# Operands of a feed-forward block's second weight matrix prepared beside the mixers instead of in the feed-forward stage, on one Trainium2 core

## The chip, the cores and the metric

The kernel runs on one core of a Trainium2 chip. The core has a matrix engine (PE, with its weight loads shown apart as PEld), a vector engine (DVE), a scalar engine (ACT), a general engine (POOL), and a sync engine (SP) that issues most of the DMAs. Each engine works through its own list of instructions in order. The metric is the device time of one execution, in microseconds (us), and lower is better.

## The reference

One decoder layer, run for a prompt of 2048 tokens behind 16 meta tokens, and for 8 sample sequences of 4 tokens, with the same weights. The mixer has three groups of heads side by side: HGRN2 (a gated linear recurrence), mLSTM, and sliding-window attention with sinks. A SwiGLU block follows.

```python
def _trunk(h, init_states, past_kvs, params):
    ...
        y, st = _mixer(_rmsnorm(h, norm_mix[l]), p, init_states[l], kv)
        h = h + y
        h = h + _swiglu(_rmsnorm(h, norm_ffn[l]), w_ffn_in[l], w_ffn_out[l])
    ...
def _swiglu(hn, w_ffn_in, w_ffn_out):
    g, u = jnp.split(hn @ w_ffn_in, 2, axis=-1)
    return (jax.nn.silu(g) * u) @ w_ffn_out
```

The model width is 1024, the inner width of the SwiGLU block is 2816, and all inputs are float32. The results are the two trunk outputs and the recurrent states of both groups.

## The kernel before

**Stages.** Tokens are worked in 17 tiles: tile 0 holds the 32 sample tokens and the 16 meta tokens, tiles 1 to 16 hold 128 prompt tokens each. For each tile `project` multiplies by the input weights, which stay in SBUF, and `mix` runs the three mixers. `mixer_prompt` (L857) takes turns between three generators, `swa_prompt`, `mlstm_prompt` and `hgrn_prompt`. In HGRN2 a chain of levels doubles its block length each time: PE products `lv` (L527), a masked copy on DVE (L540), and updates of `qz` and `k` on DVE (L549, L551). After the tiles come the output product, the sample group's mixer and the norm of the feed-forward block. Then follow three groups of six tiles (the third with the short tile 0 and four others) through the SwiGLU block.

**Numbers as pairs.** A float32 operand is held as a sum of two float16 values: `split_w` (L154 to L156) writes the high part on ACT and the low part on DVE, and a product takes three float16 passes (`PASSES`).

**Seven products for eight.** The SwiGLU block uses a Strassen-like scheme: a 2 by 2 block product with seven products and sums of blocks. A unit of 256 columns of weights is therefore seven operands, each as a float16 pair, 896 KB in all. The sums are four subtractions or additions on POOL (`left` L1012 for the first matrix, `right` L1020 for the second), and the split takes three calls of `split_w` (`operands`).

**Group 0 makes, groups 1 and 2 load.** In the first group (6 buffers `w`) `kept` (L1127) makes a unit from the raw weights and stores it to a DRAM scratch (L1134); in the other groups (11 buffers) it loads it from there (L1136). There are 44 units of the first matrix (`gu_operands`, raw loads L1186) and 22 of the second (`dn_operands`, raw loads L1198, scratch `wdn_scratch`).

**Inside a group.** The 11 inner blocks `jq` are taken in four parts of 2, 3, 3 and 3 (`PARTS`). `hidden` does the gate and the up product of a block (`quad`, PE products L1239; POOL sums L1248, L1249), then the product of the two (DVE L1262) and the block sums (POOL L1274 to L1280), and writes the pairs `hh` (ACT L1268, DVE L1269). `down` (PE products L1292) needs the `hh` of a whole part and the units of the second matrix, `m` = 0 and 1, and adds to `xr`. In the first two parts of group 0 `prep_late` also prepares the inputs of the last tiles.

**Order.** The instructions are written in program order; a scheduler with a timeline of its own then places each on its engine's list, earlier where it judges the operands ready and the engine free. Buffers from pools bound how far: a new tile of a tag waits until the oldest one of that tag is released. DMAs on SP are a list like any other.

**Sample group.** Tile 0's projection leaves the sample group's results (`s_q`, `s_k`, `s_cin` and so on, in `tl` and beside it) in SBUF tiles of their own until the sample mixer reads them after tile 15.

**Masks.** Seven masks `lv`, 64 wide, are made by two `affine_select` each (L406, L407).

## Time and profile before

| | |
|---|---|
| median of 3 runs | 2424.07 us (2414.37 to 2427.03) |
| profiled execution, its own time | 2414.44 us |
| span of its trace | 2412.7 us |
| granted PE clock, mean | 0.97 |
| mixers of tiles 1 to 15 | about 100 to 784 us of the span |
| SwiGLU group 0, first to last PE product | 1055.3 to 1595.9 us |
| SwiGLU group 1 | 1602.1 to 2056.4 us |
| SwiGLU group 2 | 2056.2 to 2394.6 us |

How to read the rows shown below. A row of a group of instructions gives line, engine, operation, output and inputs with their shapes, then count, busy time in us, mean duration in ns, and the engine's idle time just before them with what ended it. A row of a table of stretches gives, after the stretch and its length, the busy us (and the count of instructions) of PE, PEld, DVE, ACT and POOL, then the granted PE clock, the share of time for which the DMA engines were busy, and GB/s. A row of waits gives who waited for whom, us in total, times, and the longest. A row of the timeline gives start, duration, engine, line and instruction, and in brackets the idle time before. Line numbers are those of the kernel before.

### The profile page before, as it was taken

Reading aid. Unit: us, or ns where it says so; the run is one execution under the profiler, and the core shown is the slowest. Engines: PE = TensorE matmul, PEld = TensorE weight load, DVE = VectorE, ACT = ScalarE, POOL = GpSimd, SP = SyncE. Lnnn points to the kernel's source line nnn. Section 1 sums busy time; section 2 is a strip of 40 time slices with the busy share of each in tenths; the row PEclk is TensorE's granted clock in tenths of the full one; section 3 lists DMA queues with packets and bytes.
Section 4 is the critical chain, followed back from the end, with each engine's and each line's share of the span. In section 5 each row is a group of like instructions: output and inputs, shape, how many; then the busy total and the mean of one; then the engine's idle time right before and its main releaser. Section 6 shows DMA issues by size and latency. Waiting matters only on the chain. (4 is left out here: it accounts for less than half of the span.)

```text
span 2412.7 us, 51978 instructions
## 1 busy us (share of the span) xinstructions
PE 2220.3 (92%) x20298; PEld 1607.4 (67%) x20298; DVE 1679.2 (70%) x4030; ACT 943.5 (39%) x2526; POOL 1211.7 (50%) x1629
## 2 busy tenths in 40 slices
PE   6989999999999899896989979889999999999996
PEld 6677767767776445444657556567686767888886
DVE  8788988988988756558879677746454535655546
ACT  7554455554554432334343434422212123332323
POOL 7344344444443464549778788744232324544435
PEclk9999999999999899997999989899999999999998
DMA  7232333333223755996436545684324247744441
GB/s 258 50 63 69 66 67 68 75 61 74 66 64 73 173 183 192 275 330 222 153 139 231 196 158 191 191 287 185 148 108 168 108 152 199 269 176 175 177 174 38
DMA packets 294329, 364.95 MB, mean 151 GB/s; under 512 B 203808, under 2 KB 234480, under 8 KB 294067
## 3 DMA queue, kind: packets, MB, share of 16 engines
q1 hardware_dynamic: 285090, 331.02, 43.6%
q0 software_dynamic: 4384, 15.93, 1.7%
q10 hardware_dynamic: 4608, 14.68, 1.7%
q8 instruction: 159, 2.61, 0.4%
q14 instruction: 88, 0.71, 0.1%
HBM read 212.24 MB, written 103.50 MB: 131 GB/s over the span
## 5 line engine op out<-in xcount | busy, mean ns | idle before, releaser
L1239 PE MATMUL s<-x,w 128*128 128x384 f16 (+1 forms) x5544 | 826.4, 312 | 14.8 <-DMA w<-wgu_scratch 6.2
L1239 PEld LDWEIGHTS <-w 128*128 128x128 f16 x5544 | 542.6, 98 | 296.5 <-issue 13.8
L1292 PE MATMUL dn<-w,hh 128*128 128x256 f16 (+1 forms) x4158 | 444.4, 278 | 56.0 <-ACT hh L1268 23.6
L1292 PEld LDWEIGHTS <-hh 128*128 128x128 f16 (+1 forms) x4158 | 379.6, 99 | 119.8 <-ACT hh L1268 27.8
L212 PEld LDWEIGHTS <-xT 128*128 128x128 f16 (+1 forms) x1992 | 177.4, 99 | 191.4 <-issue 25.2
L1268 ACT ACTIVATE hh<-tmp 128x384 f16<-128x384 f32 (+1 forms) x231 | 112.4, 494 | 280.4 <-DVE tmp L1262 164.5
L1248 POOL TENSOR_TENSOR tmp<-tmp,tmp 128x384 f32<-128x384 f32 (+1 forms) x66 | 65.3, 990 | 279.0 <-ACT tmp L1247 271.8
L1269 DVE TENSOR_TENSOR hh<-tmp,hh 128x384 f16<-128x384 f32 (+1 forms) x231 | 144.5, 633 | 74.2 <-ACT hh L1268 72.5
L212 PE MATMUL wo<-wo,xT 128*128 128x512 f16 x768 | 180.8, 394 | 9.5 <-DVE xn L992 4.6
L156 DVE SCALAR_TENSOR_TENSOR w<-raw,w 128x512 f16<-128x512 f32 (+1 forms) x136 | 111.9, 855 | 7.0 <-ACT w L155 6.9
L1250 DVE TENSOR_TENSOR tmp<-s,tmp 128x384 f32<-128x384 f32 (+1 forms) x66 | 34.2, 518 | 107.3 <-PE s L1239 107.3
L212 PE MATMUL d<-xT,qf 128*128 128x128 f16 (+1 forms) x1632 | 107.7, 220 | 0.0
L156 DVE SCALAR_TENSOR_TENSOR w<-sums,w 128x1024 f16<-128x1024 f32 x68 | 96.9, 1427 | 11.4 <-ACT w L155 11.4
L1259 ACT ACTIVATE tmp<-tmp 128x384 f32<-128x384 f32 (+1 forms) x132 | 61.6, 489 | 107.9 <-DVE tmp L1250 52.6
L212 PE MATMUL d<-xT,bqk 128*128 128x128 f16 (+1 forms) x1632 | 100.6, 221 | 3.2 <-DVE e L278 3.2
L1324 DVE SCALAR_TENSOR_TENSOR xr<-dn,xr 128x256 f32<-128x256 f32 x192 | 78.7, 417 | 34.4 <-PE dn L1292 30.2
L212 PEld LDWEIGHTS <-qf 128*128 128x128 f16 x1632 | 94.4, 100 | 9.1 <-issue 4.1
L212 PEld LDWEIGHTS <-bqk 128*128 128x128 f16 x1632 | 94.0, 100 | 5.4 <-issue 4.5
L212 PE MATMUL d<-xT,cq 128*128 128x128 f16 (+1 forms) x1632 | 96.2, 217 | 0.0
L212 PE MATMUL d<-bvo,xT 128*128 128x512 f16 (+1 forms) x408 | 96.2, 380 | 0.0
L1262 DVE SCALAR_TENSOR_TENSOR tmp<-tmp,tmp 128x384 f32<-128x384 f32 (+1 forms) x132 | 71.9, 558 | 34.1 <-POOL tmp L1249 32.6
L212 PE MATMUL d<-aig,xT 128*128 128x512 f16 (+1 forms) x408 | 92.4, 379 | 3.4 <-DVE g L358 3.4
(536 smaller groups left out, 4064.6 us busy)
## 6 DMA issues: line engine op xcount, KB each, us to landing
w<-wgu_scratch SPq DMA_DIRECT2D x88, 896.0 KB
wgu_scratch<-w SPq DMA_DIRECT2D x44, 896.0 KB
w<-wdn_scratch SPq DMA_DIRECT2D x44, 896.0 KB
raw<-in_w_ffn_in_dram SPq DMA_DIRECT2D x88, 256.0 KB
...
xs<-in_x_prompt_dram SPq DMA_DIRECT2D x26, 512.0 KB
...
raw<-in_w_ffn_out_dram SPq DMA_DIRECT2D x22, 512.0 KB
```

Of the source, the lines that this page charges most:

```text
L156: V.scalar_tensor_tensor(lo, src, scale, hi, op0=ALU.mult, op1=ALU.subtract)
L212: T.matmul(out, lh(k, a), rh(k, b), start=(n == 0), stop=(n == 3 * nk - 1))
L1239: T.matmul(out, A[k // 2][p][:, a, k % 2 * P : k % 2 * P + P], x2[r][:, k // 2, op, k % 2, :n], start=i == 0, stop=i == 11)
L1248: G.tensor_tensor(r12, r12, r22, op=ALU.add)
L1250: V.tensor_tensor(r11, prod(A12, B21), r11, op=ALU.add)
L1259: S.activation(d, d, AF.Silu, scale=UF)
L1262: V.scalar_tensor_tensor(d, v, UF * HS, d, op0=ALU.mult, op1=ALU.mult)
L1268: S.activation(hi, v, AF.Copy)
L1269: V.tensor_tensor(lo, v, hi, op=ALU.subtract)
L1292: T.matmul(out, hh[p][:, q, a, off : off + L], ws[q][r][:, b], start=(q, p, r) == order[0], stop=(q, p, r) == order[-1])
L1324: V.scalar_tensor_tensor(x[:L, cc], m, UD, x[:L, cc], op0=ALU.mult, op1=ALU.add)
```

## The change

The units of the second matrix are no longer made in group 0. They are cut into 44 pieces of half a unit (`wdn_scratch` gets one more axis), and a new generator `dn_prep(4)` runs as a fourth beside the three mixers in tiles 4 to 14. Each piece is loaded raw one piece ahead (three DMAs into a tile `nr`, two buffers), goes through four POOL subtractions into `ns` (one buffer) and two `split_w` calls into `nw` (one buffer), and is stored by one DMA. In all three SwiGLU groups `dn_operands` now loads a unit with two DMAs, and PE reads it as two runs of 128 columns.

To make room, the sample group's projections are written into tiles of the tags `nr`, `ns` and `nw`, stored to a new DRAM scratch after tile 0's projection (`put_away`, five DMAs) and loaded again before the sample mixer (`take_back`, five DMAs). The tile `tg` now shares the tag of `xq`. Five masks `lv`, 32 wide, replace the seven; each takes two `affine_select` into a scratch tile `dm` and two copies.

```diff
-    wdn_d = nc.dram_tensor("wdn_scratch", (NFF // 2, 2, P, 2 * 7 * 256), F16, kind="Internal").ap()
+    wdn_d = nc.dram_tensor("wdn_scratch", (NFF // 2, 2, 2, P, 2 * 7 * P), F16, kind="Internal").ap()
+    smp_d = nc.dram_tensor("smp_scratch", (4, P, 512), F32, kind="Internal").ap()
...
+    def pack():
+        packed[:] = [at_("nr", [P, 512], bufs=2), at_("nr", [P, 512], bufs=2), at_("ns", [P, 512]), at_("nw", [P, 896])]
...
+    def put_away():
+        for which, n, c0, c1 in SPK_PARTS:
+            nc.sync.dma_start(smp_d[which, :n, c0:c1], packed[which][:n, c0:c1])
+
+    def take_back(s):
+        pack()
+        for which, n, c0, c1 in SPK_PARTS:
+            nc.sync.dma_start(packed[which][:n, c0:c1], smp_d[which, :n, c0:c1])
+        for tag in SPK:
+            setattr(s, tag, in_pack(tag))
...
             if s.name == "s":
-                return at_("s_" + tag, shape, dt)
+                if not packed:
+                    pack()
+                return in_pack(tag)
...
-                tg = at_("tg", [P, 256])
+                tg = at_("xq", [P, 256])
...
+        if t == 0:
+            put_away()
         yield
...
-    for li in range(7):
+    for li in range(5):
         h = 1 << li
-        m = at_(f"lv{li}", [P, 64])
+        m = at_(f"lv{li}", [P, 32])
+        z = am_("dm", [P, 64])
...
+        for u in range(2):
+            G.tensor_copy(m[u * 64 : u * 64 + 64], z[u * 64 : u * 64 + 64, u * 32 : u * 32 + 32])
...
-    def mixer_prompt(s, yT, off):
+    def mixer_prompt(s, yT, off, *others):
         y = zt("y", [P, 512])
-        interleave(swa_prompt(s, yT, off), mlstm_prompt(s, y[:, 256:512]), hgrn_prompt(s, y[:, 0:256]))
+        interleave(swa_prompt(s, yT, off), mlstm_prompt(s, y[:, 256:512]), hgrn_prompt(s, y[:, 0:256]), *others)
         finish_y(y, yT, off, s.L)
+
+    dn_pieces = [(jq, m, u) for jq in range(NFF // 2) for m in range(2) for u in range(2)]
+    dn_raw = []
+
+    def dn_load():
+        if dn_pieces:
+            jq, m, u = dn_pieces.pop(0)
+            x = at_("nr", [P, 4, P], bufs=2)
...
+            nc.sync.dma_start(x[:, 0], rows[0][:, 1])
+            nc.sync.dma_start(x[:, 1], rows[0][:, 0])
+            nc.sync.dma_start(x[:, 2:4], rows[1])
+            dn_raw.append((x, wdn_d[jq, m, u]))
+
+    def dn_prep(n):
+        if not dn_raw:
+            dn_load()
+            yield
+        for _ in range(n):
+            x, dst = dn_raw.pop(0)
+            dn_load()
+            yield
+            b12, b11, b21, b22 = (x[:, i] for i in range(4))
+            s = at_("ns", [P, 4, P])
+            w = at_("nw", [P, 2, 7, P], F16)
+            G.tensor_tensor(s[:, 0], b12, b11, op=ALU.subtract)
+            G.tensor_tensor(s[:, 1], b22, s[:, 0], op=ALU.subtract)
+            G.tensor_tensor(s[:, 2], b22, b12, op=ALU.subtract)
+            G.tensor_tensor(s[:, 3], b21, s[:, 1], op=ALU.subtract)
+            split_w(x[:, 1:4], w[:, 0, 0:3], w[:, 1, 0:3], WS)
+            yield
+            split_w(s, w[:, 0, 3:7], w[:, 1, 3:7], WS)
+            nc.sync.dma_start(dst, w.rearrange("p a o c -> p (a o c)"))
+            yield
...
-            mixer_prompt(seg_of[t][0], yT, 0)
+            mixer_prompt(seg_of[t][0], yT, 0, *([dn_prep(4)] if 4 <= t < 15 else []))
...
+    take_back(sseg)
     smp = sample_mixer(tc, nc, I, O, locals())
...
     def dn_operands(jq, m):
-        def make(w):
-            raw = raw_tile()
...
-            right(w, sum_tile(), raw[:, 0], raw[:, 1], raw[:, 2], raw[:, 3], raw.rearrange("p (k h) c -> p h k c", k=2)[:, 0], WS)
-        return kept(wdn_d[jq, m], make)
+        w = w_full().rearrange("p a o c -> p (a o c)").rearrange("p (u z) -> p u z", u=2)
+        for u in range(2):
+            nc.sync.dma_start(w[:, u], wdn_d[jq, m, u])
+        return w.rearrange("p u (r o c) -> p u r o c", r=2, o=7)
...
-                T.matmul(out, hh[p][:, q, a, off : off + L], ws[q][r][:, b], start=(q, p, r) == order[0], stop=(q, p, r) == order[-1])
+                T.matmul(out.rearrange("t (u c) -> t u c", u=2), hh[p][:, q, a, off : off + L], ws[q][:, :, r, b], start=(q, p, r) == order[0], stop=(q, p, r) == order[-1])
```

What the scheduler makes of it is seen in the engines' lists. First POOL's list in group 0 of the SwiGLU block, at the end of the fourth part's products, before the change: L1249 is the second sum of the last gate product, L1248 the first of the last up product, L1274 and the next lines the block sums of `hidden`, and L1022 to L1025 the subtractions of a unit of the second matrix.

```order
L1249 TENSOR_TENSOR tmp_21519<-tmp_21519,tmp_21518 128x384
L1022 TENSOR_TENSOR sums_22127<-raw_22125 128x256
L1024 TENSOR_TENSOR sums_22127<-raw_22125 128x256
L1023 TENSOR_TENSOR sums_22127<-raw_22125,sums_22127 128x256
L1022 TENSOR_TENSOR sums_22142<-raw_22140 128x256
L1024 TENSOR_TENSOR sums_22142<-raw_22140 128x256
L1025 TENSOR_TENSOR sums_22127<-raw_22125,sums_22127 128x256
L1023 TENSOR_TENSOR sums_22142<-raw_22140,sums_22142 128x256
L1025 TENSOR_TENSOR sums_22142<-raw_22140,sums_22142 128x256
L1248 TENSOR_TENSOR tmp_21657<-tmp_21657,tmp_21659 128x384
L1249 TENSOR_TENSOR tmp_21659<-tmp_21659,tmp_21658 128x384
L1274 TENSOR_TENSOR tmp_21656<-tmp_21517,tmp_21519 128x384
```

The same place of POOL's list in the changed kernel, where L1321, L1322 and L1347 are the lines that were L1248, L1249 and L1274:

```order
L1321 TENSOR_TENSOR tmp_22001<-tmp_22001,tmp_22003 128x384
L1322 TENSOR_TENSOR tmp_22003<-tmp_22003,tmp_22002 128x384
L1321 TENSOR_TENSOR tmp_22141<-tmp_22141,tmp_22143 128x384
L1322 TENSOR_TENSOR tmp_22143<-tmp_22143,tmp_22142 128x384
L1347 TENSOR_TENSOR tmp_22140<-tmp_22001,tmp_22003 128x384
```

At this place no preparation stands any more between the sums of the gate product and those of the up product, and in the second, third and fourth part POOL's list goes from the sums of `hidden` straight to those of `down`.

Next DVE's list in the mixer of tile 4, before the change: the rows of the mLSTM stabiliser (`mb`, `mr`, `rows`) with `es` and `kx` of the attention, and a level of HGRN2 (`att`).

```order
L673 CAST mb_74_473<-mrow_4338 4x128
L821 TENSOR_TENSOR es_4365<-ng_4355,sink_457 128x8
L771 COPY mst_4544<-rows_72_471 4x1
L350 SCALAR_TENSOR_TENSOR kx_4959<-d_4910,kx_4959 64x128
L674 TENSOR_TENSOR mr_4381<-mrow_4338,mb_74_473 4x128
L675 CAST mb_74_473<-mr_4381 4x128
L676 TENSOR_TENSOR mb_74_473<-mr_4381,mb_74_473 4x128
L540 COPY_PREDICATED att_4227<-lv_43_375,lv_4343 64x4x8x4 x2
```

The same place of DVE's list in the changed kernel (L714 to L717 were L673 to L676), with L158, the low parts of a piece:

```order
L715 TENSOR_TENSOR mr_4407<-mrow_4361,mb_77_482 4x128
L323 TENSOR_SCALAR f_5660<-dd_5655 128x256
L716 CAST mb_77_482<-mr_4407 4x128
L360 SCALAR_TENSOR_TENSOR qlo_5864<-d_5765,qx_730_5862 64x512
L717 TENSOR_TENSOR mb_77_482<-mr_4407,mb_77_482 4x128
L158 SCALAR_TENSOR_TENSOR nw_9633<-nr_9050,nw_9633 128x384
L158 SCALAR_TENSOR_TENSOR nw_9633<-ns_9632,nw_9633 128x512
L815 TENSOR_SCALAR kd_4602<-pairm_438,kd_4602 4x2
```

The piece stands in tile 4's stretch, although the program writes it beside a later tile: counted over DVE's whole list, by the row of `ng` (L816 before, L857 now) that each tile has once, the 44 pieces lie 1, 4, 5, 7, 7, 5, 7, 7 and 1 in the stretches that end with the `ng` row of tile 0, 1, 2 and so on to 8. The scheduler has moved them ahead of tiles 4 to 14.

Last, SP's list in the same tile of the changed kernel: the two transposes of the attention's probabilities (`pT`, L877 for the high part and L879 for the low), which followed each other before as L836 and L838.

```order
L877 DMA_TRANSPOSE pT_4397<-ph_4396 128x8x128
L914 DMA nr_9852<-in_w_ffn_out_dram 128x128
L915 DMA nr_9852<-in_w_ffn_out_dram 128x128
L916 DMA nr_9852<-in_w_ffn_out_dram 128x2x128
L937 DMA wdn_scratch<-nw_9779 128x1792
L879 DMA_TRANSPOSE pT_4397<-ph_4396 128x8x128
```

Three raw loads and a store, each with waits of its own, now stand between them.

More of the change, by code (lines that the diff above doesn't have):

```diff
@@ L217, in trunk, with in_pack @@
         pass
+    SPK = {"q": (0, 0, 64), "k": (0, 64, 64), "f": (0, 128, 64), "cin": (0, 192, 224), "ck": (0, 416, 32), "cq": (1, 0, 128),
+           "cv": (1, 128, 128), "va": (1, 256, 256), "ga": (2, 0, 256), "gb": (2, 256, 256), "vb": (3, 0, 260), "g": (3, 260, 8)}
+    SPK_PARTS = ((0, P, 0, 448), (1, P, 0, 128), (1, NS, 128, 512), (2, NS, 0, 512), (3, NS, 0, 268))
+    SHAPES = {"q": (P, 2, NS), "k": (P, 2, NS), "f": (P, 2, NS), "cin": (P, 4, NB, 7), "cq": (P, 4, NS), "ck": (P, NS),
+              "cv": (NS, P), "g": (NS, 8), "va": (NS, 256), "ga": (NS, 256), "gb": (NS, 256), "vb": (NS, 4, 65)}
+    packed = []
+    def pack():
+        packed[:] = [at_("nr", [P, 512], bufs=2), at_("nr", [P, 512], bufs=2), at_("ns", [P, 512]), at_("nw", [P, 896])]
+    def in_pack(tag):
+        which, o, n = SPK[tag]
+        shape = SHAPES[tag]
+        v = packed[which][: shape[0], o : o + n]
+        if len(shape) == 3:
+            return v.rearrange("p (a b) -> p a b", a=shape[1])
+        return v.rearrange("p (a b c) -> p a b c", a=shape[1], b=shape[2]) if len(shape) == 4 else v
+    def put_away():
[7 more added lines that the diff above has]
+            setattr(s, tag, in_pack(tag))
     def project(t, s_out):
@@ L299, in project @@
                 if s.name == "s":
-                    s.cin = at_("s_cin", [P, 4, NB, 7])
+                    s.cin = in_pack("cin")
+                    G.memset(s.cin, 0.0)
                     S.activation(s.cin[:, :, :, 3:7], pv[:, :, sl].rearrange("p j (b t) -> p j b t", t=NT), AF.Copy, scale=US)
@@ L382, in project @@
                 if s.name == "s":
-                    s.vb = at_("s_vb", [NS, 4, 65])
+                    s.vb = in_pack("vb")
                     V.memset(s.vb[:, :, 64:65], 1.0)
@@ L401, in trunk @@
     lv = []
-    for li in range(7):
+    for li in range(5):
         h = 1 << li
-        m = at_(f"lv{li}", [P, 64])
+        m = at_(f"lv{li}", [P, 32])
+        z = am_("dm", [P, 64])
         nb = 64 // h
-        G.affine_select(out=m, in_=ones[:, :64], pattern=[[-2 * h, nb], [0, h]], compare_op=ALU.is_ge, fill=0.0, base=0, channel_multiplier=1)
-        G.affine_select(out=m, in_=m, pattern=[[2 * h, nb], [0, h]], compare_op=ALU.is_ge, fill=0.0, base=h - 1, channel_multiplier=-1)
+        G.affine_select(out=z, in_=ones[:, :64], pattern=[[-2 * h, nb], [0, h]], compare_op=ALU.is_ge, fill=0.0, base=0, channel_multiplier=1)
+        G.affine_select(out=z, in_=z, pattern=[[2 * h, nb], [0, h]], compare_op=ALU.is_ge, fill=0.0, base=h - 1, channel_multiplier=-1)
+        for u in range(2):
+            G.tensor_copy(m[u * 64 : u * 64 + 64], z[u * 64 : u * 64 + 64, u * 32 : u * 32 + 32])
         lv.append(m.bitcast(I32))
@@ L855, in put_yT @@
         V.scalar_tensor_tensor(lo, pv, scale, hi, op0=ALU.mult, op1=ALU.subtract)
-    def mixer_prompt(s, yT, off):
+    def mixer_prompt(s, yT, off, *others):
         y = zt("y", [P, 512])
-        interleave(swa_prompt(s, yT, off), mlstm_prompt(s, y[:, 256:512]), hgrn_prompt(s, y[:, 0:256]))
+        interleave(swa_prompt(s, yT, off), mlstm_prompt(s, y[:, 256:512]), hgrn_prompt(s, y[:, 0:256]), *others)
         finish_y(y, yT, off, s.L)
+    dn_pieces = [(jq, m, u) for jq in range(NFF // 2) for m in range(2) for u in range(2)]
[4 more added lines that the diff above has]
+            x = at_("nr", [P, 4, P], bufs=2)
+            rows = [w_dn[(2 * jq + k) * P : (2 * jq + k + 1) * P, m * 512 : m * 512 + 512].rearrange("p (h u c) -> p h u c", h=2, u=2)[:, :, u] for k in range(2)]
+            nc.sync.dma_start(x[:, 0], rows[0][:, 1])
[22 more added lines that the diff above has]
+            yield
     def finish_y(y, yT, off, L):
```

8 lines of the change are left out of this document (3 added, 5 removed).

## The prediction

> **What bounds the kernel now.** I read the page first (PE busy 92% of the span), then the table of stretches for the three SwiGLU groups. Groups 0 and 1 have the same products on the same shapes, and differ in that group 0 makes the weight units and group 1 loads them. The first two rows are these groups, the other eight the `down` blocks of their four parts, group 0's first.
>
> ```profile
> core 0: us, PE busy (x) PEld busy (x) DVE busy (x) ACT busy (x) POOL busy (x), PEclk, DMA share, GB/s
> 1055.30:1595.90 540.60, 477.00 (x3243) 322.55 (x3241) 414.14 (x631) 222.10 (x440) 422.37 (x437) 0.94 0.57 196
> 1602.10:2056.40 454.30, 454.01 (x3236) 317.06 (x3237) 220.44 (x428) 107.42 (x233) 153.72 (x176) 1.00 0.47 168
> ...
> 1111.80:1167.40 55.60, 35.66 (x253) 26.61 (x254) 51.16 (x77) 20.72 (x42) 50.84 (x52) 0.75 0.56 204
> 1252.90:1309.00 56.10, 47.21 (x378) 39.09 (x378) 54.18 (x82) 23.12 (x49) 48.00 (x50) 0.91 0.65 234
> 1397.70:1456.30 58.60, 45.97 (x381) 37.97 (x379) 48.26 (x81) 18.52 (x40) 47.45 (x50) 0.88 0.47 172
> 1540.70:1595.90 55.20, 45.52 (x380) 37.90 (x377) 39.98 (x75) 19.52 (x49) 34.18 (x44) 0.88 0.83 203
> 1658.50:1686.90 28.40, 28.11 (x256) 24.63 (x254) 23.76 (x54) 6.89 (x17) 16.69 (x20) 1.00 0.35 131
> 1768.60:1810.00 41.40, 41.40 (x380) 37.08 (x379) 25.11 (x54) 7.11 (x17) 16.30 (x20) 1.00 0.30 112
> 1891.80:1933.20 41.40, 41.40 (x381) 37.05 (x380) 25.11 (x53) 7.11 (x17) 16.30 (x20) 1.00 0.30 112
> 2014.90:2056.40 41.50, 41.50 (x382) 37.17 (x380) 27.83 (x57) 13.66 (x37) 22.50 (x34) 1.00 0.96 239
> ```
>
> Group 1 is bound by PE, which never rests. Group 0 takes 540.6 - 454.3 = 86.3 us more for the same count of products. Of these 225.5 - 152.7 = 72.8 us lie in the `down` blocks: 27.2, 14.7, 17.2 and 13.7; the other 13.5 us lie in the gate and up products and the seams. The timeline at the start of the fourth `down` shows why.
>
> ```profile
> 1541.82 1.11 POOL L1022 TENSOR_TENSOR sums<-raw 128x256 f32<-128x256 f32 x1 [1.80 <-DVE w L156]
> ...
> 1548.57 0.72 POOL L1025 TENSOR_TENSOR sums<-raw,sums 128x256 f32<-128x256 f32 x1
> 1549.25 0.99 POOL L1248 TENSOR_TENSOR tmp<-tmp,tmp 128x384 f32<-128x384 f32 x1
> 1550.32 0.99 POOL L1249 TENSOR_TENSOR tmp<-tmp,tmp 128x384 f32<-128x384 f32 x1
> 1551.35 0.56 DVE L1262 SCALAR_TENSOR_TENSOR tmp<-tmp,tmp 128x384 f32<-128x384 f32 x1 [4.12 <-POOL tmp L1249]
> 1552.43 0.82 PE L1292 MATMUL dn<-w,hh 128*128 128x256 f16 x3 [3.55 <-DVE hh L1269]
> ```
>
> Two units of the second matrix hold POOL from 1541.8 to 1549.3; the sums of the up product (L1248, L1249) queue behind them, DVE's L1262 waits for those, and PE for `hh`. PE does not lack weights here: it lacks `hh`, because the preparation stands ahead of it in POOL's list.
>
> **Term 1: group 0 loses its 22 units.** Rows of group 0 price a unit.
>
> ```profile
> L1022 POOL TENSOR_TENSOR sums<-raw 128x256 f32<-128x256 f32 x22 | 24.9, 1131 | 26.1 <-DVE w L156 26.1
> L1024 POOL TENSOR_TENSOR sums<-raw 128x256 f32<-128x256 f32 x24 | 21.9, 913 | 0.0
> L156 DVE SCALAR_TENSOR_TENSOR w<-raw,w 128x256 f16<-128x256 f32 x64 | 46.3, 724 | 0.0
> L156 DVE SCALAR_TENSOR_TENSOR w<-raw,w 128x512 f16<-128x512 f32 x64 | 61.8, 966 | 6.9 <-ACT w L155 6.9
> L156 DVE SCALAR_TENSOR_TENSOR w<-sums,w 128x1024 f16<-128x1024 f32 x64 | 91.0, 1423 | 8.0 <-ACT w L155 8.0
> L155 ACT ACTIVATE w<-raw 128x512 f16<-128x512 f32 x64 | 39.5, 617 | 29.7 <-DMA raw<-in_w_ffn_in_dram 18.1 <-PE dn L1292 10.2 <-DVE w L1152 1.5
> ```
>
> POOL: four rows of 0.91 to 1.13, about 4 us a unit, 22 x 4 = 88 us of its 422. DVE: 0.72 + 0.97 + 1.42 = 3.11, 68 us of its 414. What stays is 44 units of the first matrix, less those made ahead of group 0. In the changed lists five of them lie inside the second and the third `down`: DVE has 25.1 us there in group 1, and 25.1 + 5 x 3.11 = 40.7 of 41.4 leaves nothing spare, so I leave 4 us of loss in each. In the first part `prep_late` and units of the first matrix still stand before `hh`: I leave 10 of 27. The fourth keeps 1, the products 2. 86.3 - 21 = **65 us gained**; between 35 (see the third rival) and 76 (only the first part's loss stays).
>
> **Term 2: the mixers take 44 pieces.** A piece is half a unit: four POOL rows of 128x128, and on ACT and DVE a row of 384 and one of 512 columns. By the count in DVE's list, 43 of the 44 lie in the stretch between the `ng` rows of tiles 0 and 8; the second row is the rest of the mixers, the third the tile with the busiest DVE.
>
> ```profile
> 81.10:436.50 355.40, 327.81 (x4162) 260.00 (x4162) 307.85 (x994) 183.59 (x627) 149.13 (x273) 0.99 0.30 67
> 436.50:760.00 323.50, 303.32 (x3824) 238.71 (x3822) 280.40 (x902) 164.18 (x554) 134.51 (x240) 1.00 0.31 67
> ...
> 256.00:301.20 45.20, 39.56 (x512) 32.57 (x511) 41.19 (x133) 22.36 (x78) 19.46 (x35) 0.96 0.33 69
> ...
> L156 DVE SCALAR_TENSOR_TENSOR w<-raw,w x136: 410/721/5095, 989.9 to 1557.8; 128x512 f16<-128x512 f32 x68, 128x256 f16<-128x256 f32 x68
> L205 DVE SCALAR_TENSOR_TENSOR yh<-y,yh 128x512 f16<-128x512 f32 x7 | 4.9, 704 | 0.4 <-ACT yh L203 0.4
> L553 POOL TENSOR_TENSOR t<-f 128x128 f32<-128x128 f32 x8 | 4.6, 570 | 6.5 <-DVE Sst L599 4.8 <-DVE k L551 1.6
> ```
>
> DVE has 355.4 - 307.9 = 47.5 us to spare there, PE 27.6. Lower price of a piece on DVE: 512 columns 0.70 (L205, in the mixers), 384 halfway from there to the least L156 (256 columns, 0.41), 0.56: 1.26. Upper price, from group 0: (0.72 + 0.97)/2 + 0.97 = 1.81. So 43 pieces are 54 to 78 us: DVE would need 362 to 386 us. ACT gets 43 x about 1.1 on 184, POOL 43 x 4 x 0.57 = 98 on 149: both stay below 70%.
>
> I take the upper price, because POOL is what lengthens such rows, and POOL goes from 42% busy to some 60%. One tile shows it: a DVE row of 128x4 values that can take 0.14 us takes 0.72 while a POOL row runs.
>
> ```profile
> 497.85 0.73 POOL L373 TENSOR_TENSOR ga<-ga,gA 128x256 f32<-128x256 f32 x1 [4.88 <-DVE pp L634]
> 497.88 0.72 DVE L635 SCALAR_TENSOR_TENSOR pp<-pp,z 128x4 f32<-128x4 f32 x1
> ...
> L635 DVE SCALAR_TENSOR_TENSOR pp<-pp,z x18: 142/161/719, 66.7 to 778.9; 128x4 f32<-128x4 f32 x16, 16x4 f32<-16x4 f32 x1, 32x4 f32<-32x4 f32 x1
> ```
>
> The Trainium skill (SBUF — State Buffer, Who interferes with whom) says that a vector instruction with two SBUF inputs and a GpSimd instruction that reads SBUF exclude each other, each for its whole length; the row of 0.72 agrees. By that rule alone the pieces would add DVE's 54 and POOL's 98 us to one shared door, an estimate of up to 152 us against what time the door is free, instead of DVE's 78.
>
> DVE's list cannot be gapless: it waits for products and for ACT. Its busiest tile has 41.2 of 45.2 us, 91%; with five to seven pieces a tile to fill gaps I take 95%. 385.7/0.95 = 406, **51 us lost**. At 100% and the lower price it would be 7, at 91% and the upper price 68.
>
> **What is hidden.** The pieces move 176 DMAs to SP in the mixers and take 44 from group 0. At 0.3 to 0.4 us each they fit beside the 14 that a tile has; transposes behind a store that waits (SP's list above) are in the 95%. Unit loads in groups 1 and 2 become two DMAs instead of one, 44 more issues, on a queue that waits anyway; the moving operand of `down` becomes two runs of 128 columns, and a product that already reads four such runs (L845) takes as long as one that reads 512 in a row.
>
> ```profile
> SPq L1136 <- PE s L1239: 416.3, 79, 12.3
> ...
> L845 PE MATMUL oc<-pT,cvx 128*64 128x512 f16 (+1 forms) x198 | 35.0, 395 | 9.5 <-DMA pT<-ph 9.4
> L212 PE MATMUL wo<-wo,xT 128*128 128x512 f16 x768 | 180.8, 394 | 9.5 <-DVE xn L992 4.6
> ...
> 1.59 2.24 POOL L406 TENSOR_SCALAR_AFFINE_SELECT lv<-ones 128x64 f32<-128x64 f32 x7 [0.21 <-DVE ones L108]
> ```
>
> The masks now need the pool that opens after the input weights, so ten selects at 2.24/7 = 0.3 us and ten copies come some 55 us later, ahead of the first tiles' levels: 0 to 5 us, I take 2. The ten DMAs of the sample group's values lie beside loads of weights; the sample mixer's first reads would wait for the last of them, and the mixers of tiles 15 and 16 cover that: 0, or a few us.
>
> **Sum**, against the profiled execution's own 2414.4 us: 2414.4 - 65 + 51 + 2 = **2402 us**. The median of the runs shown is 9.7 above that execution, which is inside the range below.
>
> **The rivals.**
>
> *The mixers absorb it.* DVE at the lower price fills its gaps: 7 to 15 us lost, and 70 gained: 2414 - 70 + 12 = **2356**. For it: 47.5 us are free, ACT and POOL are half idle, and PE, at 92% of the stretch, may hold the pace. Against it: the pieces crowd into eight tiles instead of eleven, with DVE past 100% at even the lower price.
>
> *Slower: DVE stands behind the single buffer `nw`.* The first ACT row of a piece has to wait until the store of the one before has landed, and DVE's next L158 waits for ACT, with the mixer's rows queued behind it. Transfers of this size landed or were waited for like this:
>
> ```profile
> h_scratch<-xs POOLq DMA_DIRECT2D x10, 512.0 KB, 5.9
> DVE pT L156 <- DMA x_scratch<-pT: 30.8, 8, 9.0
> ```
>
> In DVE's changed list I added up the mean durations of the rows between one piece's last L158 and the next one's first: in 20 of 43 places they come to less than 6 us, 58 us short in all. If none of that falls into waits that DVE has anyway, the stretch becomes 386 + 58 = 444, 88 us longer: 2414 - 65 + 88 + 2 = **2439**. The point from which it decides: 63 us in the mixers, 1.5 us a piece.
>
> *Group 0 stays late.* The 44 units of the first matrix and `prep_late` keep POOL and DVE ahead of `hh`, so that only 35 us come back, half of the `down` loss: 2414 - 35 + 51 + 2 = **2432**. Against it: the lists are clean before the second to fourth `down`.
>
> **Chances.** The forecast (2390 to 2415) 0.48, absorbed 0.20, behind `nw` 0.20, group 0 late 0.12. About 12 us (0.5%) is what a measurement of this kernel can tell from no change. Faster by more, below 2402: half of the forecast's, nearly all of the first rival's, 0.43. Within: 0.33. Slower, above 2426: the other two for the most part, 0.24. The range reaches into both sides: 2356 to 2442, which leaves out half of the first rival and a quarter of the second and third.
>
> **What would show it.** Right: the four `down` blocks of group 0 at some 38, 45, 45 and 43 us, and the stretch of tiles 1 to 8 at some 406 us with DVE at 95%; tiles 9 to 15 unchanged. The first rival shows that stretch below 370 us, the second shows ACT or DVE rows of `nw` waiting for DMA `wdn_scratch<-nw`, the third shows PE L1292 waiting for `hh` as now. Wrong altogether: products of `down` longer than in group 1 now, or a start of tile 0 later by more than 5 us.

## The result, and the profile after

| | before | changed |
|---|---|---|
| median of 4 runs each | 2425.55 us (2414.37 to 2427.92) | 2458.9 us (2454.2 to 2461.67) |
| ratio to before, 95% interval | | 1.0155 [1.0131, 1.0179] |
| profiled execution, its own time | 2414.44 us | 2457.16 us |

The change makes the kernel 1.6% slower; faster was forecast. The table of stretches of the changed kernel answers to the one of before: first the mixers up to the `ng` row (now L857) of tile 8, then to that of tile 15, then the stage up to group 0; then groups 0 and 1, and group 0's four `down` blocks.

```profile
core 0: us, PE busy (x) PEld busy (x) DVE busy (x) ACT busy (x) POOL busy (x), PEclk, DMA share, GB/s
83.60:508.70 425.10, 368.75 (x4368) 292.87 (x4366) 366.15 (x1095) 231.53 (x726) 244.46 (x448) 0.94 0.50 132
508.70:854.50 345.80, 318.64 (x3811) 243.98 (x3810) 273.55 (x917) 169.03 (x566) 141.56 (x248) 0.99 0.35 73
854.50:1157.00 302.50, 233.77 (x1518) 126.24 (x1515) 180.08 (x411) 93.81 (x246) 154.84 (x215) 0.84 0.68 195
1157.00:1637.10 480.10, 461.20 (x3243) 319.04 (x3241) 339.56 (x559) 180.41 (x368) 312.09 (x333) 0.98 0.56 188
1644.60:2099.30 454.70, 454.18 (x3236) 317.09 (x3237) 219.49 (x427) 107.45 (x233) 152.51 (x175) 1.00 0.48 167
1211.60:1254.70 43.10, 33.50 (x255) 26.19 (x254) 38.88 (x69) 15.03 (x32) 34.59 (x38) 0.88 0.44 156
1344.00:1388.10 44.10, 43.79 (x380) 38.12 (x381) 30.53 (x57) 10.47 (x23) 24.34 (x28) 0.95 0.56 204
1469.80:1511.70 41.90, 41.59 (x381) 37.00 (x379) 36.05 (x63) 12.78 (x28) 28.63 (x32) 1.00 0.42 148
1593.50:1637.10 43.60, 41.71 (x379) 36.73 (x377) 27.60 (x56) 13.89 (x37) 22.27 (x34) 1.00 1.05 214
```

Group 0 is what was hoped for: 480.1 us instead of 540.6, its `down` blocks at 43.1, 44.1, 41.9 and 43.6 us. From group 0's first product to the last product of the trace the changed kernel takes 58.7 us less (1280.6 instead of 1339.3 us). But group 0 starts 101.7 us later (1157.0 instead of 1055.3). Of these, 2.5 us come ahead of the first `ng`, and 69.7 us in the first stretch (425.1 instead of 355.4), which holds 43 of the 44 pieces. Another 22.3 us come in the tiles behind it (345.8 instead of 323.5), which **hold no piece at all**, and 7.2 us in the stage up to group 0 (302.5 instead of 295.3, the row of which was this):

```profile
760.00:1055.30 295.30, 257.57 (x1728) 136.45 (x1726) 188.52 (x435) 102.85 (x265) 144.08 (x212) 0.92 0.69 201
```

DVE's waits show what is new. First the kernel before, then the changed one, both from 60 to 930 us of the span.

```profile
DVE num L707 <- PE n L766: 13.7, 9, 6.4
DVE dm L698 <- PE sc L696: 7.2, 5, 2.3
```

```profile
DVE dm L739 <- PE sc L737: 33.8, 14, 8.1
DVE num L748 <- PE n L807: 31.3, 10, 5.3
DVE nw L158 <- ACT nw L157: 25.2, 15, 4.1
```

The piece's own wait (`nw`) is there, 25.2 us. The larger part is that DVE waits 65.1 us, not 20.9, for two products of mLSTM, `sc` and `n`. The place matters, though. These are the first rows of the same view for the first stretch of the changed kernel alone (83.6 to 508.7 us), which holds the pieces:

```profile
DVE nw L158 <- ACT nw L157: 21.1, 14, 3.7
DVE dm L739 <- PE sc L737: 6.8, 5, 2.1
DVE qz L544 <- PE oa L631: 6.4, 4, 2.6
DVE num L748 <- PE n L807: 3.7, 3, 1.5
```

There `sc` and `n` make 10.5 us (6.2 before), and the piece's own wait is the larger one. Most of the rest of the 65.1 us, 46.5 us, lies behind the `ng` row of tile 8 (508.7 to 917 us). The timeline of the changed kernel in a tile without pieces shows what PE does meanwhile:

```profile
572.13 4.70 PE L214 MATMUL d<-aig,xT 128*128 128x512 f16 x21
576.75 0.40 PE L886 MATMUL oc<-pT,cvx 128*64 128x512 f16 x1
577.09 0.72 PE L737 MATMUL sc<-qk 64*128 64x128 f32 x8
577.83 0.76 DVE L739 TENSOR_TENSOR dm<-sc,dm 128x256 f32<-128x256 f32 x2 [3.61 <-PE sc L737]
...
578.78 3.19 PE L214 MATMUL d<-bvo,xT 128*128 128x512 f16 x14
581.80 0.33 PE L744 MATMUL n<-vb,dm 128*128 128x65 f32 x2
581.97 0.44 PE L807 MATMUL n<-Cst,qk 128*128 128x130 f32 x2
...
583.34 0.43 DVE L748 TENSOR_TENSOR num<-n,ex 128x260 f32<-128x260 f32 x1 [3.92 <-PE n L807]
```

PE works through projection products (`d`, L214), and the small products that DVE needs stand behind them. So the next view counts projections. These are PE's rows of `d` from the start to the `ng` row of tile 10: before, then changed.

```profile
0.00:529.20 529.20, 358.17 (x4481) 34.43 (x92) 51.43 (x145) 0.99 0.35 88
```

```profile
0.00:610.30 610.30, 388.64 (x4845) 36.98 (x100) 56.38 (x157) 0.95 0.50 132
```

A tile has 384 such products (6528 in 17 tiles). Tiles 0 to 10 need 4224; before, 257 of tile 11 were done too, 0.67 of a tile; now 621, **1.62 tiles ahead**. Counted in the same way at the other tiles, the projections of the changed kernel are 0.5 to 1.2 of a tile further ahead than before from tile 3 to tile 14, and at tiles 0 to 2 less than 0.2.

### The profile page after: what moved, and what is told of

The parts are those of the page before. It is cut to its first block, busy times and chain, and to the rows that moved or that the text cites. A ratio compares the mean times of both kernels' runs of the same rounds, so it can differ in the third digit from the quotient of the medians.

```text
span 2455.4 us, 52512 instructions
## 1 busy us (share of the span) xinstructions
PE 2241.8 (91%) x20298; PEld 1634.0 (67%) x20298; DVE 1649.8 (67%) x4052; ACT 945.9 (39%) x2548; POOL 1218.7 (50%) x1724
## 5 line engine op out<-in xcount | busy, mean ns | idle before, releaser
L1365 PE MATMUL dn<-w,hh 128*128 128x256 f16 (+1 forms) x4158 | 430.7, 275 | 20.1 <-DVE w L1231 6.8
L214 PEld LDWEIGHTS <-xT 128*128 128x128 f16 (+1 forms) x1992 | 182.9, 102 | 233.9 <-issue 54.5
L214 PE MATMUL wo<-wo,xT 128*128 128x512 f16 x768 | 185.1, 401 | 41.9 <-DVE xs L1076 22.5
L1321 POOL TENSOR_TENSOR tmp<-tmp,tmp 128x384 f32<-128x384 f32 (+1 forms) x66 | 65.3, 990 | 296.5 <-ACT tmp L1320 281.8
L214 PE MATMUL d<-xT,qf 128*128 128x128 f16 (+1 forms) x1632 | 108.8, 225 | 5.7 <-DVE g L393 4.5
L214 PEld LDWEIGHTS <-qf 128*128 128x128 f16 x1632 | 98.4, 103 | 11.4 <-issue 5.3
L1399 POOL TENSOR_TENSOR tmp<-tmp,tmp 128x256 f32<-128x256 f32 (+1 forms) x72 | 54.6, 758 | 97.1 <-ACT tmp L1378 48.9
L214 PE MATMUL d<-aig,xT 128*128 128x512 f16 (+1 forms) x408 | 94.3, 384 | 3.2 <-DVE g L393 3.2
L214 PE MATMUL d<-xT,bqk 128*128 128x128 f16 (+1 forms) x1632 | 96.2, 219 | 0.6 <-DVE e L312 0.6
L214 PE MATMUL d<-bvo,xT 128*128 128x512 f16 (+1 forms) x408 | 93.8, 379 | 2.3 <-DVE qlo L360 2.3
L878 POOL TENSOR_TENSOR ph<-pb,ph 128x1024 f16<-128x1024 f32 (+1 forms) x34 | 71.3, 2096 | 46.3 <-ACT ph L876 41.2
L214 PE MATMUL d<-xT,cq 128*128 128x128 f16 (+1 forms) x1632 | 93.7, 217 | 0.0
L1402 POOL TENSOR_TENSOR tmp<-tmp,tmp 128x256 f32<-128x256 f32 (+1 forms) x72 | 58.9, 818 | 69.7 <-DVE xr L1401 69.7
L568 PE MATMUL lv<-qz,k 128*64 128x64 f32 (+2 forms) x848 | 60.0, 246 | 35.9 <-DVE k L592 33.3
```

What stands on the lines that cost most here:

```text
L214: T.matmul(out, lh(k, a), rh(k, b), start=(n == 0), stop=(n == 3 * nk - 1))
L568: T.matmul(ps[c, i * w : (i + 1) * w].rearrange("p (a b h) -> p a b h", a=2, h=h), s.k[:, i, c], qz[:, i, :, c].rearrange("p a (b w h) -> ...
L878: G.tensor_tensor(lo.rearrange("p (g k) -> p g k", g=4), pb, hi.rearrange("p (g k) -> p g k", g=4), op=ALU.subtract)
L1321: G.tensor_tensor(r12, r12, r22, op=ALU.add)
L1365: T.matmul(out.rearrange("t (u c) -> t u c", u=2), hh[p][:, q, a, off : off + L], ws[q][:, :, r, b], start=(q, p, r) == order[0], stop=(q, ...
L1399: G.tensor_tensor(u2, u2, m5, op=ALU.add)
```

## The experiments

Two theories stood at first: the pieces' own rows fill DVE's list (the forecast), or the single buffer `nw` makes ACT and DVE wait for landing stores (the second rival). The third, that something besides the pieces costs, came from the tiles without pieces. Times of one run are read against the kernel before, measured beside them (2419.09, 2424.37, 2424.21 us for each four in turn; 2420.32 us for the last four).

### 1 to 4: no pieces, a free buffer, no POOL, pieces in order

**1.** `dn_prep` keeps only its stores (from a tile of zeros).

```diff
-            G.tensor_tensor(s[:, 0], b12, b11, op=ALU.subtract)
...
-            split_w(s, w[:, 0, 3:7], w[:, 1, 3:7], WS)
-            nc.sync.dma_start(dst, w.rearrange("p a o c -> p (a o c)"))
+            nc.sync.dma_start(dst, dn_zero[0].rearrange("p a o c -> p (a o c)"))
```

> The changed kernel without the work of a piece: no raw loads, no subtractions on POOL, no splits on ACT and DVE; the 44 stores stay and write a tile of zeros, so the SwiGLU block reads zeros as its second matrix. Packing, shared tags, masks and the new layout stay. Theory A (pieces cost the time where they stand, tiles 0 to 8, and nothing else does): the first product of group 0 comes 70 us earlier than in the changed kernel (1157 us), but tiles 9 to 16 and the stage behind them keep their 30 us, total about 2388 us. Theory B (all of the loss comes from the pieces, the later tiles are late because of them too): group 0 starts at about 1055 to 1060 us, total about 2358 us. Theory C (packing, shared tags and masks cost the most): group 0 starts later than 1110 us, total above 2410 us. The products of group 0 should take as long as in the changed kernel.

Measured: 2412.2 us, group 0 starts at 1114.3 us: the numbers of theory C, and the surprise of the study. (Its reason, the room that was made, is tried by itself in experiment 5.) Without any work of a piece group 0 still starts 59 us later than before. All 44 stores stand between 80 and 137 us in SP's list, PE is 1.67 tiles of projection ahead at tile 10, and DVE waits 87.8 us for `sc` and `n`.

**2.** The stores read the resident input weights instead of `nw`.

```diff
-            nc.sync.dma_start(dst, w.rearrange("p a o c -> p (a o c)"))
+            nc.sync.dma_start(dst[:, 0:1024], wp["qf"][0][0].rearrange("p k c -> p (k c)"))
+            nc.sync.dma_start(dst[:, 1024:1792], wp["qf"][0][1].rearrange("p k c -> p (k c)")[:, 0:768])
```

> The changed kernel, with the stores of the pieces read from the resident input weights (two DMAs of the same total size) instead of nw, so that nw is free again as soon as DVE has written it and no store waits for DVE; the second matrix then holds wrong values. Theory A (the lists of DVE and PE are simply fuller by the pieces' rows): no change beyond 8 us against 2457 us. Theory B (the single buffer nw: ACT waits 40 us for landing stores and DVE 25 us for ACT): these two waits vanish, the stretch of tiles 1 to 8 falls from 425 to about 385 to 400 us, total about 2420 to 2432 us.

Measured: 2419.6 us, group 0 at 1114.2 us. Theory A is out. Theory B is right in the total and in little else: the stretch of tiles 1 to 8 takes 414.4 us, not 385 to 400, and DVE still waits 23.0 us for ACT's `nw`, 18.5 of them ahead of the first piece. It doesn't settle the case: the lead of the projections went as well (0.65 of a tile), so two things changed at once. The tiles without pieces, from the `ng` row of tile 8 to that of tile 15, lose nothing here: 320.2 us, 323.5 before.

**3.** The four subtractions are left out, both splits read `nr`.

> The changed kernel without the four POOL subtractions of a piece: both splits read the raw tile, so the second matrix holds wrong values. ACT, DVE, loads and stores stay. Theory A (POOL's rows and DVE's exclude each other, so POOL's 88 us of subtractions lengthen DVE's rows): the stretch of tiles 1 to 8 becomes 20 to 40 us shorter, total 2420 to 2437 us. Theory B (the single buffer nw and the 54 us of rows on DVE): within 10 us of 2457 us, as ACT still waits for the stores.

Measured: 2434.1 us, in all inside theory A's range, though the stretch of tiles 1 to 8 is only 15 us shorter (85.3 to 495.5 us). The lead stays (1.55 tiles), group 0 starts at 1138.2 us. Why this gains 23 us while the pieces are hoisted, and 1 us once they are in order (experiment 10), stays open; up to group 0 the same 2628 rows of DVE are 15.4 us shorter in all (871.0 us, 886.4 in the changed kernel).

**4.** The first POOL and the first ACT row of a piece keep their place in program order.

```diff
-            G.tensor_tensor(s[:, 0], b12, b11, op=ALU.subtract)
+            tc.keep_in_program_order(G.tensor_tensor(s[:, 0], b12, b11, op=ALU.subtract))
...
-            split_w(x[:, 1:4], w[:, 0, 0:3], w[:, 1, 0:3], WS)
+            tc.keep_in_program_order(S.activation(w[:, 0, 0:3], x[:, 1:4], AF.Copy, scale=WS))
+            V.scalar_tensor_tensor(w[:, 1, 0:3], x[:, 1:4], WS, w[:, 0, 0:3], op0=ALU.mult, op1=ALU.subtract)
```

> The changed kernel, with the first POOL and the first ACT row of each piece pinned behind what is written before them on their engine, so that four pieces stand in each of the tiles 4 to 14 instead of five to seven in the tiles 1 to 7. Nothing is left out. Theory A (the pieces crowd: with four a tile DVE needs 40 + 5 us of a tile's 46): the mixers lose 10 to 25 us instead of 98, total about 2370 to 2385 us. Theory B (the order of the lists in the later tiles is what the packing and the shared tags disturb): the 30 us of the tiles 9 to 16 stay, total about 2400 us. Theory C (a piece costs about 2 us wherever it stands): total within 15 us of 2457 us.

Measured: 2413.5 us, group 0 at 1103.6 us: 44 us less than the changed kernel, with the same work, less than theory A hoped and 13 us above theory B's 2400. The lead is 0.82 of a tile, the waits for `sc` and `n` 9.1 us.

### 5 and 6: is it the room that was made, or the order?

**5.** The kernel before with the packing, the shared tag and the masks alone.

> The kernel before with only the edits that make room: the sample projections packed, put away and taken back, tg in the tag of xq, the five masks. The second matrix is made in group 0 as before, nothing is left out. Theory A (making room costs nothing; the first experiment's 59 us came from the lists that were reordered around its burst of stores): group 0 starts at 1055 to 1065 us, total 2412 to 2425 us. Theory B (the shared tags and the packing tie projections and mixers together, whatever the pieces do): group 0 starts at 1100 to 1115 us, total 2465 to 2480 us.

Measured: 2419.0 us beside 2424.4 for the kernel before, group 0 at 1060.2 us. Theory A: making room costs nothing that one execution of each can show.

**6.** As experiment 1, with each store pinned on SP.

```diff
-            nc.sync.dma_start(dst, dn_zero[0].rearrange("p a o c -> p (a o c)"))
+            tc.keep_in_program_order(nc.sync.dma_start(dst, dn_zero[0].rearrange("p a o c -> p (a o c)")))
```

> As the first experiment (no raw loads, subtractions or splits; 44 stores of zeros, so the SwiGLU block reads zeros as its second matrix), but each store pinned behind what is written before it on SP, so that four stand in each of the tiles 4 to 14. Theory A (room costs nothing, the burst of stores disturbed the lists): group 0 starts at 1055 to 1070 us, total 2355 to 2370 us. Theory B (the shared tags and the packing cost some 50 us): total 2405 to 2415 us, as in the first experiment.

Measured: 2363.3 us, group 0 at 1060.8 us. The same instructions as in experiment 1, in another order, are 49 us faster; and 2363 us is what the change would bring if a piece cost nothing.

### 7 to 12: the price of a piece, and the projections pinned

**7.** Experiment 4 with two tags in place of `nw` (`nwa` for the first split, `nwb` for the second), each stored as soon as it is written.

> The fourth experiment (pieces in program order, 2413.5 us) with nw cut into two tags, one for each split, each stored by a DMA of its own as soon as it is written; the same SBUF, nothing left out. Theory A (ACT's 37 us of waits for landing stores are on the path): the mixers lose 15 to 30 us less, total 2385 to 2400 us. Theory B (in order, the 1.24 us that a piece takes on DVE set the price, the waits for stores lie beside DVE's rows): within 6 us of 2413 us.

Measured: 2406.4 us, 7 less than experiment 4, just below theory B's range and well above theory A's. Executions of this one kernel lie between 2402 and 2415 us (experiment 16), so the 7 us are not clear of noise, and the stores' landing is a small part at most.

**8.** Experiment 7 with the low part of the first split on POOL.

> The experiment with two tags, with the low part of the first split (128x384) made on POOL: POOL first scales the raw tile in place, then subtracts the high part; DVE is rid of 44 x 0.55 = 24 us, POOL gets some 90 us more. Nothing left out. Theory A (DVE's rows set the price of a piece): 15 to 25 us less than with two tags alone. Theory B (POOL's rows and DVE's hinder each other, or POOL's queue delays the mixers' rows): no gain, or up to 30 us more.

Measured: 2416.9 us, 10 more. Theory B: a POOL row of 128x384 takes 0.91 us there, and DVE's gain is lost.

**9.** The changed kernel, with the projections pinned.

```diff
-        interleave(project(t, seg_of[t]))
+        with tc.issue_after(last_oc[max(last_oc) - 1].ins):
+            interleave(project(t, seg_of[t]))
```

> The changed kernel, pieces hoisted as there, with one thing pinned: the PE products of the projection of tile t stand behind the last product of the sliding-window attention of tile t-2. In the changed kernel's trace 1.6 tiles of projection are done beyond a tile when its ng comes, in the kernel before 0.6. Nothing left out. Theory A (the lists run the projections a tile too far ahead, which fills the early tiles and leaves the last mixers without cover; this is the 50 us that the first experiment lost without any piece): group 0 starts at 1100 to 1120 us, total 2400 to 2420 us. Theory B (the crowded pieces and the waits for nw are what is lost): total 2440 to 2465 us.

Measured: 2438.0 us, group 0 at 1135.0 us. The lead is gone (0.65), so are the waits for `sc` and `n` (14.7 us), and from tile 10 to tile 14 a tile takes 44.5 to 46.5 us, as before. But tiles 1 to 9, beside which the pieces stand, stay at 53 to 60 us each. Between A and B: 22 us of the late start go with the lead.

**10.** Experiment 7 without the subtractions.

> The experiment with pieces in order and two tags (2406 us) without the four POOL subtractions of a piece; both splits read the raw tile, so the second matrix holds wrong values. Theory A (DVE's 1.24 us a piece are the price): within 6 us of 2406 us. Theory B (POOL's 1.84 us a piece lengthen DVE's rows or delay POOL's own): 2376 to 2391 us.

Measured: 2405.4 us, 1.0 less. Theory A's number: in order, POOL's subtractions cost nothing that one execution can show. DVE's rows are shorter without them all the same, as is shown further down.

**11.** Experiment 7 with ACT rows in the place of DVE's two.

> The experiment with pieces in order and two tags (2406 us) with DVE's two rows of a piece taken away: ACT writes the high part a second time in their place, so the low parts hold wrong values. Theory A (DVE's 1.24 us a piece are the price): 2363 to 2381 us, most of the 43 us between 2406 us and the kernel without pieces (2363 us) come back. Theory B (any work in the mixers' lists costs, or POOL's): 2390 to 2410 us.

Measured: 2394.2 us, 12.2 less, inside theory B's range. DVE's rows are a part of the price, not most of it. ACT's rows are doubled here, so the 12.2 us are what is left after whatever the added ones cost, which was not measured.

**12.** Experiment 7 with the projections pinned.

> The experiment with pieces in order and two tags, with the projections pinned as well. When ng comes, 0.8 of a tile of projection is done ahead there, little more than in the kernel before. Theory A (the lead costs only where it is a whole tile too long): within 8 us of 2406 us. Theory B (each tenth of a tile of lead costs 4 to 5 us): 2385 to 2398 us.

Measured: 2434.0 us, **27.5 more**; neither theory. The pin itself does harm: it cuts the lead at tiles 1 to 5 to 0.26 to 0.43 of a tile, from 0.93 to 1.02 in experiment 7. So experiment 9's gain is a net of two things, and its size says little.

### 13 to 16: one pin, and what beats both kernels

**13.** The changed kernel with one pin, on the store; `nw` stays single.

```diff
-            nc.sync.dma_start(dst, w.rearrange("p a o c -> p (a o c)"))
+            tc.keep_in_program_order(nc.sync.dma_start(dst, w.rearrange("p a o c -> p (a o c)")))
```

> The changed kernel with one edit: the store of a piece on SP is pinned behind what is written before it there, so that the single buffer nw itself keeps the next pieces from being hoisted. Nothing else is pinned, nothing left out. Theory A (the hoisting is the cause of half the loss: it crowds the pieces and lets the lists of the projections run a tile ahead): projections 0.5 to 0.9 of a tile ahead when ng comes, total 2400 to 2420 us. Theory B (the waits at nw are the cause): total above 2440 us, since nw is as single as before.

Measured: 2404.0 us, ratio to the kernel before 0.9931 [0.9906, 0.9955]; group 0 starts at 1102.5 us. This run decides between the order and the single buffer. ACT's waits for the landing store, in the changed kernel and then in experiment 13:

```profile
ACT nw L157 <- DMA wdn_scratch<-nw: 40.1, 19, 7.7
```

```profile
ACT nw L157 <- DMA wdn_scratch<-nw: 32.3, 19, 7.0
DVE nw L158 <- ACT nw L157: 9.2, 9, 3.9
DVE num L748 <- PE n L807: 6.2, 4, 4.6
DVE dm L739 <- PE sc L737: 3.0, 2, 1.9
```

ACT waits for the single buffer as often as in the changed kernel, 32 us instead of 40, and 55 us are gone all the same: theory A. What went is most of DVE's wait for `sc` and `n` (9.2 us instead of 65.1), of its wait for `nw` (9.2 instead of 25.2) and of the lead (0.83 of a tile instead of 1.62).

**14.** Two tags, with only the two stores pinned.

> Two tags for nw as in the seventh experiment, but with only the stores pinned on SP, not the POOL and ACT rows. Nothing left out. Theory A (an order near the written one is enough, whoever is pinned): 2398 to 2412 us. Theory B (the pins on POOL and ACT cost something themselves): 2385 to 2397 us.

Measured: 2407.3 us, ratio 0.9948 [0.9930, 0.9966]: theory A, whoever is pinned.

**15.** Experiment 6 with the raw loads as well.

> As the sixth experiment (stores of zeros in order, 2363 us), with the raw loads of the pieces as well, pinned in order; no subtractions or splits, so the SwiGLU block reads zeros as its second matrix. Theory A (of a piece only its rows on the engines cost): 2358 to 2370 us. Theory B (its loads delay the mixers' transposes, and are the half of its price that DVE's rows don't explain): 2375 to 2390 us.

Measured: 2376.5 us, 13.2 more than experiment 6, group 0 at 1075.3 us. Theory B's range: the loads are about a third of a piece's price. Its mechanism is seen, though not shown to be the whole: from 60 to 930 us ACT waits 34.7 us for the transposes `pT` (26.6 in experiment 6) and 31.7 us for the transposes `xT` (18.2).

**16.** Experiment 7 again.

> The seventh experiment again (pieces in order, two tags for nw), timed in rounds. If its one time of 2406 us holds: ratio to the kernel before 0.990 to 0.997.

Measured: 2407.1 us, ratio 0.9948 [0.9930, 0.9966].

### The experiments side by side

Four of them make a square: a piece's work present or not, its stores hoisted or in order. The start of group 0 is read from the first of PE's rows of `quad`; in this view of one line's rows the two times behind the durations are the first and the last start. The rows are of experiment 6, experiment 1, experiment 13 and the changed kernel.

```profile
L1303 PE MATMUL s<-x,w x5544: 282/326/527, 1060.8 to 2311.4; 128*128 128x384 f16 x132, 128*128 128x280 f16 x66
```

```profile
L1303 PE MATMUL s<-x,w x5544: 282/326/527, 1114.3 to 2360.4; 128*128 128x384 f16 x132, 128*128 128x280 f16 x66
```

```profile
L1312 PE MATMUL s<-x,w x5544: 282/326/528, 1102.5 to 2357.5; 128*128 128x384 f16 x132, 128*128 128x280 f16 x66
```

```profile
L1312 PE MATMUL s<-x,w x5544: 282/326/528, 1157.0 to 2405.5; 128*128 128x384 f16 x132, 128*128 128x280 f16 x66
```

In order, the pieces' work costs 1102.5 - 1060.8 = 41.7 us. Without any work, the hoisting costs 1114.3 - 1060.8 = 53.5 us. Together that is 1156.0, and the changed kernel starts group 0 at 1157.0 us. **The two costs add up to the whole loss, and the larger one is the order.** The agreement within 1 us is in part luck: experiments 7 and 16 are the same program, and start group 0 at 1102.4 and 1097.7 us.

The same can be read in PE's own time. These rows of the table of stretches run from the start of the span to group 0's first product, in the kernel before, experiment 6, experiment 1, experiment 13 and the changed kernel.

```profile
0.00:1055.30 1055.30, 951.70 (x10589) 684.73 (x10590) 841.49 (x2534) 502.15 (x1568) 476.45 (x802) 0.97 0.44 115
0.00:1060.80 1060.80, 958.04 (x10588) 686.11 (x10589) 841.46 (x2534) 501.02 (x1568) 476.21 (x810) 0.97 0.49 133
0.00:1114.30 1114.30, 973.87 (x10588) 702.68 (x10589) 821.01 (x2540) 502.10 (x1574) 504.50 (x826) 0.94 0.48 131
0.00:1102.50 1102.50, 979.02 (x10588) 713.65 (x10589) 903.57 (x2622) 542.24 (x1656) 574.97 (x985) 0.95 0.51 138
0.00:1157.00 1157.00, 988.74 (x10589) 714.82 (x10590) 886.41 (x2628) 546.20 (x1662) 593.58 (x1001) 0.93 0.51 136
```

The products are the same. Of the 101.7 us that the changed kernel loses there, PE is idle for 64.7 us more, and for 37.0 us more it is busy with the same products, at a granted clock of 0.93 instead of 0.97. Hoisting empty stores (experiment 1 beside 6) adds 37.7 us of idle and 15.8 us of busy time, the pieces' work in order (13 beside 6) 20.7 and 21.0. Whether the lower clock only follows from PE's waits or is a cost of its own was not tried.

The lead and DVE's waits, by the same views as above:

| kernel | projections ahead at tile 10 | DVE waits for `sc` and `n` | group 0 starts |
|---|---|---|---|
| before | 0.67 | 20.9 us | 1055.3 us |
| 5, room alone | 0.67 | 25.5 | 1060.2 |
| 6, stores in order | 0.56 | 16.3 | 1060.8 |
| 7, two tags, in order | 0.82 | 13.2 | 1102.4 |
| 13, store pinned | 0.83 | 9.2 | 1102.5 |
| 4, in order | 0.82 | 9.1 | 1103.6 |
| 2, free `nw`, hoisted | 0.65 | 9.2 | 1114.2 |
| 9, projections pinned, hoisted | 0.65 | 14.7 | 1135.0 |
| 1, stores hoisted, no pieces | 1.67 | 87.8 | 1114.3 |
| 3, no subtractions, hoisted | 1.55 | 57.5 | 1138.2 |
| changed | 1.62 | 65.1 | 1157.0 |

The three kernels with the long lead are the three with the long waits. The loss behind tile 8 goes with the lead: in experiments 2 and 9, hoisted but without it, the tiles without pieces take as long as before. How the 53.5 us divide between the lead and the crowding of the pieces into tiles 0 to 8 stays open: experiment 2 has the crowding without the lead and is 12 us behind experiment 13, experiment 9 is 33 us behind it, but with a pin that harms (experiment 12). Why the scheduler puts the projections earlier was not tried. A burst of stores on SP is not enough: in experiment 2 the 88 stores stand between 23 and 107 us, and the lead is 0.65.

## Why the prediction was wrong

**Term 1, group 0: right, a little large.** 65 us were forecast; group 0 takes 60.5 us less, and 58.7 are left at the end of the trace. The `down` blocks were put at 38, 45, 45 and 43 us, and are 43.1, 44.1, 41.9 and 43.6; the first keeps more loss, and in all they keep 20.0 us for the 19 left to them. The products and seams keep 5.8 us, not 2. The third rival (group 0 stays late) is out.

**Masks and packing: right.** 2 us were forecast; experiment 5 starts group 0 4.9 us later than the kernel before and is not slower in all. The new layout of `down` costs nothing, as forecast: group 1 takes 454.7 us, 454.3 before. One count of the prediction is short: for the 44 DMAs that leave group 0, 44 loads of units come in there too.

**Term 2, the mixers: wrong, and it decides.** The step that failed is the assumption that moved pieces add their own rows and leave the other rows where they were ("tiles 9 to 15 unchanged"). In the place of 51 us the mixers and the stage behind them lost 101.7. In the terms of the sum: with DVE's busy time as measured, the 95% would have made the first stretch 366.2/0.95 = 385.4 us, 30.0 more than before. It took 425.1, another 39.7 us, and 32.0 us were lost where the forecast put nothing (2.5 ahead of the first `ng`, 22.3 and 7.2 behind tile 8). The count of pieces in the lists was right, 43 of 44 ahead of tile 8. But the same lists also held the projections a tile earlier, and they were read for the pieces alone. Experiments 1 and 6 price that order at 53.5 us without a single piece.

Inside the first stretch two sizes were off in opposite directions. These groups of the changed kernel are DVE's rows of the pieces from 70 to 480 us:

```profile
L158 DVE SCALAR_TENSOR_TENSOR nw<-ns,nw 128x512 f16<-128x512 f32 x44 | 31.3, 711 | 2.8 <-ACT nw L157 2.8
L158 DVE SCALAR_TENSOR_TENSOR nw<-nr,nw 128x384 f16<-128x384 f32 x44 | 26.8, 609 | 22.4 <-ACT nw L157 22.3
```

A piece takes 0.71 + 0.61 = 1.32 us of DVE, near the lower price of 1.26 us; 1.81 was taken, for POOL's sake. DVE's busy time grew by 58.3 us (366.2 - 307.9), not 78. But DVE is busy for 366.2 of 425.1 us, 86%, not 95%: its idle time was to shrink from 47.5 to some 20 us, and grew to 58.9. What is new in it is the 21.1 us behind ACT's `nw`. On balance no row of a piece filled a gap. Nor are the rows all that the stretch lost: in experiment 1, with no row of a piece, it takes 32.0 us more than in experiment 6 (390.7 and 358.7, each by its own `ng` rows).

**The rule on the shared door.** The reason for the upper price was that POOL lengthens DVE's rows, and by the rule of the Trainium skill (SBUF — State Buffer, Who interferes with whom) the prediction made an estimate of up to 152 us of shared time. The exclusion is seen in single rows of the changed kernel. Here a DVE row of 128x384, which takes 0.55 us elsewhere, starts 0.57 us behind a POOL row and takes 1.98 us:

```profile
359.30 2.14 POOL L878 TENSOR_TENSOR ph<-pb,ph 128x1024 f16<-128x1024 f32 x1
359.87 1.98 DVE L158 SCALAR_TENSOR_TENSOR nw<-nr,nw 128x384 f16<-128x384 f32 x1
```

And a POOL subtraction that starts just behind a DVE row of a piece (at 140.44 us) takes 0.82 us, where most take 0.46. For the rows of a piece this is rare. Of the 44 rows of 128x384, 23 ran for the most part beside a POOL row and 21 beside none: their medians are 0.558 and 0.551 us. All 88 rows of the pieces take 58.1 us, 3.7 more than at the medians of those beside no POOL row (0.551 and 0.685 us). For DVE's rows in all it is more. These rows run to group 0 in experiment 7 and in experiment 10, which takes 90 us of POOL rows away:

```profile
0.00:1102.40 1102.40, 980.07 (x10588) 709.26 (x10589) 910.86 (x2622) 542.19 (x1656) 579.21 (x985) 0.95 0.51 138
0.00:1097.80 1097.80, 978.61 (x10589) 708.88 (x10589) 887.64 (x2622) 540.96 (x1656) 488.96 (x809) 0.95 0.52 139
```

DVE's 2622 rows take 23.2 us less without POOL's 90 us, so POOL does lengthen them, by a quarter of its own time, and the whole gains 1.0 us. In order, the exclusion is therefore not what sets the time. In the hoisted order experiment 3 gained 23 us, and what the exclusion has in that was not taken apart.

**The second rival came nearest by number (2439 us) and is a part of the loss at most.** Its waits exist, ACT 40.1 and DVE 25.2 us, and DVE's are the new ones of the first stretch. But with the buffer free (experiment 2) that stretch is only 10.7 us shorter, and experiment 13 keeps the single buffer, still has 32.3 us of ACT's waits, and is 55 us faster than the changed kernel. DVE's own waits for `nw` fall to 9.2 us there, so most of ACT's no longer hold DVE up.

**The price of a piece in order** is 41.7/44 = 0.95 us. It is made of several parts: the raw loads (0.3 us, experiment 15), DVE's rows (at least 0.28, experiment 11), and nothing that shows for POOL's subtractions (experiment 10). DVE's busy time alone does not set it, since experiment 10 has 23 us less of that. These are differences of single executions, and 5 us of scatter are 0.1 us a piece. The rest, presumably ACT's rows, was not taken apart.
